# A two-layer attention encoder: order of the gate product, the raw keys' scaling and the second score halves in layer A

## The chip, the cores and the metric

The kernel runs on one core of a Trainium2 chip. The core has a matmul engine (TensorE, PE in the profile; its weight loads are shown apart as PEld), three engines for elementwise work (VectorE or DVE, ScalarE or ACT, GpSimd or POOL), and SyncE (SP), on whose queue nearly all DMA transfers of this kernel are issued. Each engine has a stream of its own instructions. Operands lie in SBUF, matmul results in PSUM. The metric is the device time of one execution in microseconds, lower is better; the median of a few runs is given.

## What is computed

The input x has 512 tokens of 1024 channels, all in float32. Two layers follow each other, each with 16 heads of 64 channels: RMS norm, one input projection to queries, keys, values and a gate, an attention, the product with silu(gate), an output projection, and the residual sum.

```
for i in range(2):
    hn = rms_norm(x, norm_gain[i])
    y = mixer_a(...) if i == 0 else mixer_b(...)
    x = x + y
```

Layer A (`mixer_a`) has three groups of queries, keys and values per head, with dilations 1, 4 and 16, and merges the three attentions by their softmax denominators; queries and keys are RMS-normalised per head. The part that matters here, for each head:

```
q = rms_norm(qkv[:, :, g, 0], q_gain[g])
k = rms_norm(qkv[:, :, g, 1], k_gain[g])
logits = einsum('...qd,...kd->...qk', q, k) * scale + bias      # masked to a window
p = exp(logits - max); out = (p @ v) / denom                    # per group g
y = sum(alpha[g] * out[g]) * silu(gate)
y @ w_out
```

Layer B (`mixer_b`) is a two-dimensional neighbourhood attention on an 8 x 64 grid of the tokens, with one group. The change does not touch it.

## The kernel before

**Precision.** The large products are made as three matmuls of a high and a low part (`mm3`): high x high, high x low, low x high. Weights come from memory in blocks `wraw`; ACT casts the high part `wh` (line 127), and DVE or POOL subtracts it to get the low part `wl` (line 131). Both have four buffers of 512 columns, and `wraw` has three of 1024. The projections use one such piece for each of the eight k-steps, 12 matmuls of 512 columns a step.

**Head pairs.** Layer A goes through eight head pairs, `hc` = 0 to 7. For each, the main stream (`main_a`) projects 512 columns with the keys and values of dilations 4 and 16 (`rawk`), then 512 columns with the three queries and the first keys (`rawq`), then the first values (`v0_a`) and the gate (`gate_a`). Evictions from PSUM are on line 458 (ACT); POOL squares, DVE sums, and `head_norm` computes the reciprocal root and multiplies the raw tile by it in place (line 295, four DVE instructions, 128x256 for `rawk`, 128x512 for `rawq`). For `rawk` the root is made on POOL (lines 108 to 120), which takes some microseconds.

**Two streams.** PE runs in an order written out by the program. A main stream yields the projections, matmul by matmul; a side stream yields the attention work (transposes, scores, product with v), and `run` puts pieces of the side stream between the projections' matmuls. A model clock (`clock`) adds up, in ticks of about a nanosecond, what PE's matmuls should take; it knows nothing of waits. The side stream says when it wants to go on: `yield 1200` means 1200 ticks later, `yield "wait", key, 5200` means 5200 ticks after the event `key` was stamped. `later_on(delay, job)` puts a job into a list of timers that `tick` starts once the model clock is there. What the program issues this way is its program order. The streams of the other engines are arranged by a planner that may move an instruction ahead of others; `keep_in_program_order` pins one behind the instruction that was issued on that engine just before it.

**The stage around the change.** Between the projections of head pair hc + 1 the side stream runs the attention of pair hc (`attn_a`), in two halves u = 0 and 1 of two query tiles each. Its order for pairs 0 to 5 ("moved" pairs) is:

- the projection `rawk` of pair hc + 1 ends and stamps its event; `normed` calls `head_norm`, which issues the root and the scaling (line 295);
- `split_q` prepares queries and keys (ACT lines 601 and 620, DVE lines 604 and 624);
- if the pair before has its product with v pending, it is taken now: `weigh` makes 48 matmuls into the tile `o`, and `put_y` multiplies the gate by it (line 673, DVE), casts the high part of y (line 679, ACT) and subtracts for the low part (line 680, POOL). This is so for hc = 1 to 5, as pair 0 has none before it;
- 5200 ticks after the stamp, `scores(0)`: 12 matmuls of the first group and 64 small ones of the other two, into four tiles "log", two for each query tile;
- softmax on DVE (lines 790, 801, 652) and ACT (lines 812, 653), then DVE transposes of the probabilities into the tile `tr` (line 725, one buffer); `send` writes `tr` to memory (line 734) and reads it back in another layout (line 738), by timers;
- 17800 ticks after the stamp, `scores(1)`, with the same behind it;
- 22500 ticks after the stamp, `k_a` transposes the normalised raw keys of pair hc + 1 on PE (tile "tp") and DVE scales them by the gains (line 525).

Pair 6 has `yield 1200` and `yield 8500` in place of the two waits, and pair 7 a path of its own. The tiles `o`, "log" and "tp" share a pool of four PSUM banks (`ps_side`, bufs=4), taken in turn, so a new tile waits until the one that had its bank is read. The projections have four other banks.

Of the kernel before, what the change touches and what calls it, by code (L numbers as in the profile page):

```python
# [26 lines left out]
NHC = 8  # L27
# [15 lines left out]
def tile_hybrid_encoder(  # L43
# [13 lines left out]
    nc = tc.nc  # L57
# [47 lines left out]
    def rsqrt(eng, r, ss, n, scale):  # L105
        v = wk.tile([P, 32], F32, tag="nv", name="nv", bufs=1)
        a = wk.tile([P, 32], F32, tag="na", name="na")
        eng.tensor_scalar(v[:, :n], ss, scale, EPS, op0=ALU.mult, op1=ALU.add)
        eng.tensor_scalar(
            r.bitcast(I32), v[:, :n].bitcast(I32), -0.5, float(0x5F3759DF), op0=ALU.mult, op1=ALU.add  # L110
        )
        for _ in range(3):
            eng.tensor_mul(a[:, :n], r, r)  # L113
            if eng is nc.vector:
                eng.scalar_tensor_tensor(a[:, :n], a[:, :n], -0.5, v[:, :n], op0=ALU.mult, op1=ALU.mult)
                eng.scalar_tensor_tensor(r, a[:, :n], 1.5, r, op0=ALU.add, op1=ALU.mult)
                continue
            eng.tensor_mul(a[:, :n], a[:, :n], v[:, :n])  # L118
            eng.tensor_scalar(a[:, :n], a[:, :n], -0.5, 1.5, op0=ALU.mult, op1=ALU.add)  # L119
            eng.tensor_mul(r, r, a[:, :n])  # L120
# [105 lines left out]
    def later_on(delay, job):  # L226

        timers.append((clock[0] + delay, job))
        timers.sort(key=lambda t: t[0])
# [46 lines left out]

    later = []

    def head_norm(raw, ss, ns, held):


        rs = wk.tile([P, 32], F32, tag="rs", name="rs")
        rsqrt(nc.vector if ns == 8 else nc.gpsimd, rs[:, : 4 * ns], ss[:, : 4 * ns], 4 * ns, 1.0 / DH)

        def scale():
            for i in range(4):
                by = rs[:, i * ns : (i + 1) * ns].unsqueeze(2)
                if len(raw.shape) == 4:
                    v = raw[:, :, i, :].rearrange("p (h a f) r -> p f h a r", h=2, f=4)
                    by = rs[:, i * ns : (i + 1) * ns].rearrange("p (f h) -> p f h", h=2)  # L290
                    by = by.unsqueeze(3).unsqueeze(4).to_broadcast([P, 4, 2, 2, 32])
                else:
                    v = raw[:, i, : ns * 64].rearrange("p (a b) -> p a b", b=64)
                    by = by.to_broadcast([P, ns, 64])
                m = nc.vector.tensor_mul(v, v, by)  # L295
                if held:
                    tc.keep_in_program_order(m)

        if held:
            later.append(scale)  # L300
        else:
            scale()

# [122 lines left out]
    def project_qk(n, ns, key, hc, guard, first=False, **kw):  # L426
# [38 lines left out]
        if first:  # L465
            st["first"] = raw, ss
            return
        normed(raw, ss, ns, key, hc)

    def normed(raw, ss, ns, key, hc):  # L470
        head_norm(raw, ss, ns, key == "raw")
        if key == "rawq" and moved(hc):
            turn_q(raw)
        st[key, hc] = raw
        stamp[key, hc] = clock[0]
# [54 lines left out]
    def turn_q(raw):  # L530

        for i in range(4):
            nc.vector.transpose(raw[:, :, i, :], raw[:, :, i, :])
# [121 lines left out]
    def put_y(hc, o, permuted, last):  # L655

        gt, rest = st.pop(("gate", hc))
        for _ in rest:
            pass
        if last and permuted:  # L660
            for c in range(4):
                q = slice(P * c, P * c + P)
                of = lambda t: t.rearrange("p (s x) -> p s x", x=16)[:, :, 4 * c : 4 * c + 4]
                nc.vector.tensor_mul(of(gt), of(gt), of(o))
                src = gt.rearrange("p (t ja x) -> p x ja t", t=4, ja=8)[:, 4 * c : 4 * c + 4]
                h, l = (t[:, hc, q].rearrange("p (x ja t) -> p x ja t", x=4, ja=8) for t in (st["y_h"], y_l))
                nc.scalar.copy(h, src)
                nc.vector.tensor_sub(l, src, h.bitcast(F32))
            return
        h, l, src = st["y_h"][:, hc, :], y_l[:, hc, :], gt  # L670
        if permuted:

            nc.vector.tensor_mul(gt, gt, o)
            src = gt.rearrange("p (t ja x) -> p x ja t", t=4, ja=8)
            h, l = (t.rearrange("p (x ja t) -> p x ja t", t=4, ja=8) for t in (h, l))
        else:
            for grid, line in ((mid_rc, mid_o), (edge_rc, edge_o)):
                nc.vector.tensor_mul(grid(gt), grid(gt), line(o))
        nc.scalar.copy(h, src)
        (nc.vector if last else nc.gpsimd).tensor_sub(l, src, h.bitcast(F32))  # L680
        stamp["ya" if permuted else "yb", hc, "y"] = 0
# [62 lines left out]
    def attn_a(hc):  # L744
# [7 lines left out]
        def scores(u):  # L752

            tiles = []
            for t in (2 * u, 2 * u + 1):
                cs, n = (64, 192) if t == 0 else (0, 192) if t == 3 else (0, 256)
                tiles.append((t, [bank("log") for _ in range(2)], cs, n))
            for t, lgs, cs, n in tiles:
                ks = slice(P * t + cs, P * t + cs + n)
                qs = slice(P * t, P * t + P)  # L760
                mm3_heads(
                    [lg[:, cs : cs + n] for lg in lgs],
                    lambda hs: q0h[hs, qs], lambda hs: q0l[hs, qs],
                    lambda hs: k0h[hs, ks], lambda hs: k0l[hs, ks], False,
                )
            for t, lgs, cs, n in tiles:
                for g in range(2):
                    for j in range(4):
                        for hd in range(2):
                            hs = slice(64 * hd, 64 * hd + 64)  # L770
                            matmul(
                                lgs[hd][32 * j : 32 * j + 32, 256 + P * g : 384 + P * g],
                                qt[hs, t, 1 + g, 32 * j : 32 * j + 32],
                                k12[hs, g, P * j : P * j + P],
                                share=2,
                                start=False,
                                stop=(g == 1),
                            )
            return [
                (hd, t, softmax(hd, t, lgs[hd], cs, n)) for t, lgs, cs, n in tiles for hd in range(2)  # L780
            ]
# [34 lines left out]
        def turn_p(hd, t, pr):  # L816
            tp = bank("tp")
            for i in range(4):
                transpose(tp[:, i * P : (i + 1) * P], pr[:, i * P : (i + 1) * P])
            dst = sb(pts[0], at(t, 0, hd, 0), [[32, 4], [512, 4], [1, 32]])  # L820
            nc.vector.tensor_copy(dst, tp.rearrange("p (i a r) -> p i a r", i=4, a=4))
# [25 lines left out]
        if hc < NHC - 1:  # L847
            for u in range(2):
                if moved(hc):
                    if pending and u == 0:  # L850
                        pending.pop(0)()
                        yield
                    yield "wait", ("rawk", hc + 1), 5200 if u == 0 else 17800
                else:
                    yield 1200 if u == 0 else 8500
                turned = turner(512)
                turners.append(turned)
                for hd, t, pr in scores(u):
                    turned.put(pr, 512, 256 * hd + 128 * (t % 2))
                send = partial(turned.send, pq[:, 2048 * u : 2048 * u + 2048], 8500, 1200)  # L860
                later_on(7000 + 2000 * u, send)
                if pending and u == 0:
                    yield 5000
                    pending.pop(0)()
            pending.append(lambda: put_y(hc, weigh(), True, False))
        else:
            for u in range(2):
                if u == 0:
                    yield "wait", ("gate", hc), 500
                yield 600  # L870
                held = scores(u)
                yield 3200
                if pending:
                    yield "wait", ("gate", hc - 1), 16800
                    pending.pop(0)()
                    yield
                for args in held:
                    turn_p(*args)
                    yield
            yield from v_a(hc)  # L880
            stamp["ya", "turned"] = 0
            put_y(hc, weigh(), True, True)
            yield

# [391 lines left out]
```

## Time and profile before

| | |
|---|---|
| median of 3 runs | 878.72 us (878.3 to 880.6) |
| profiled execution, as timed | 881.69 us |
| its span, first to last instruction | 879.9 us |
| mean granted PE clock | 0.984 |
| DMA, mean over the span | 161 GB/s |

The profiled execution is a run of its own, a little slower than the three. In the page's map of 40 slices one digit stands for 22 us; layer A fills the slices up to about 600 us, layer B the rest. "PEclk" is the clock that was granted to PE, as a share of full speed. In rows of waits, `X <- Y: a, n, m` means that instructions of X stood idle until Y had finished, for a us in total, n times, at most m us.

### The profile page before, as it was taken

The numbers are of one execution on the slowest core, as the hardware profiler recorded it, in microseconds if no ns is written. First come the engines' busy times: TensorE is split into PE (matmuls) and PEld (weight loads), VectorE is DVE, ScalarE is ACT, GpSimd is POOL, SyncE is SP. The second block draws the span as 40 slices with busy tenths as digits, with TensorE's granted clock in tenths as the row PEclk, the third lists the DMA queues.
The fourth block names the chain that finished last, engine by engine and source line by source line (L and its number), as shares of the span: only waits on it lengthen the run. The fifth ranks groups of instructions, "written<-read, shape, count | busy, mean of one in ns | idle before, by whom it ended". The sixth has DMA issues, their size and how long they took to land.

```text
span 879.9 us, 15373 instructions
## 1 busy us (share of the span) xinstructions
PE 855.7 (97%) x5547; PEld 711.0 (81%) x5547; DVE 522.9 (59%) x1335; ACT 430.6 (49%) x924; POOL 304.9 (35%) x493
## 2 busy tenths in 40 slices
PE   8999999899899899899999999999999999999998
PEld 6788878688688688688778778788988988889786
DVE  6354684574666567468357674538566666666743
ACT  7433654452652462463354543536366546665541
POOL 2252432442442432414414314112443345433511
PEclk9999999899999999999999999999999999999999
DMA  6346288268368358448638364156235655546223
GB/s 242 108 134 195 78 252 241 87 188 260 86 195 267 98 172 245 144 135 223 202 128 220 124 182 144 49 172 198 87 93 167 177 157 167 165 132 195 95 89 128
DMA packets 65372, 141.23 MB, mean 161 GB/s; under 512 B 5904, under 2 KB 23248, under 8 KB 65296
## 3 DMA queue, kind: packets, MB, share of 16 engines
q1 hardware_dynamic: 65008, 140.24, 52.2%
q8 instruction: 44, 0.72, 0.3%
q14 instruction: 32, 0.26, 0.1%
q10 hardware_dynamic: 288, 0.01, 0.0%
HBM read 109.11 MB, written 31.12 MB: 159 GB/s over the span
## 4 chain that ended last, share of the span: by engine, by line
PE 84%; DVE 5%; ACT 4%; POOL 3%; DMA 2%; issue 1%; SPq 0%; ACTq 0%; POOLq 0%; DVEq 0%
PE acc L206 72%; PE log L206 5%; PE tp L210 3%; PE o L206 3%; ACT rawk L458 2%; DVE rawk L295 1%; DMA qd<-rawq 1%; ACT p L1065 1%; POOL na L118 1%; ACT p L653 1%; POOL na L113 1%; DMA qt<-qd 1%; DMA hg<-in_head_gain 1%; POOL na L119 0%; POOL rs L120 0%
## 5 line engine op out<-in xcount | busy, mean ns | idle before, releaser
L127 ACT CAST wh<-wraw 128x512 fp32r<-128x512 f32 (+1 forms) x276 | 162.1, 588 | 304.8 <-PE acc L206 258.6
L206 PE MATMUL acc<-wh,hn_h 128*128 128x512 f32 (+1 forms) x768 | 297.0, 387 | 2.1 <-ACT wh L127 1.2
L206 PE MATMUL acc<-wl,hn_h 128*128 128x512 f32 (+1 forms) x768 | 288.0, 375 | 0.7 <-DVE wl L131 0.7
L206 PE MATMUL acc<-wh,hn_l 128*128 128x512 f32 (+1 forms) x768 | 288.1, 375 | 0.0
L131 POOL TENSOR_TENSOR wl<-wraw,wh 128x512 fp32r<-128x512 f32 (+1 forms) x110 | 136.8, 1243 | 367.4 <-ACT wh L127 337.3
L131 DVE TENSOR_TENSOR wl<-wraw,wh 128x512 fp32r<-128x512 f32 (+1 forms) x166 | 114.9, 693 | 156.3 <-ACT wh L127 151.9
L206 PEld LDWEIGHTS acc<-wh,hn_h 128*128 128x128 f32 x768 | 146.2, 190 | 31.4 <-issue 6.2
L206 PEld LDWEIGHTS acc<-wh,hn_l 128*128 128x128 f32 x768 | 145.8, 190 | 21.3
L206 PEld LDWEIGHTS acc<-wl,hn_h 128*128 128x128 f32 x768 | 146.4, 191 | 20.3 <-DVE wl L131 1.0
L206 PE MATMUL acc<-hn_h,wh 128*128 128x512 f32 x192 | 77.1, 402 | 1.6 <-ACT rawq L458 1.4
L206 PE MATMUL acc<-hn_l,wh 128*128 128x512 f32 x192 | 74.9, 390 | 0.0
L206 PE MATMUL acc<-hn_h,wl 128*128 128x512 f32 x192 | 74.9, 390 | 0.0
L653 ACT ACTIVATE p<-p,mn 128x512 f32<-128x512 f32 (+3 forms) x128 | 69.3, 586 | 0.0
L812 ACT ACTIVATE p<-p,mn 128x512 f32<-128x512 f32 (+1 forms) x64 | 44.8, 701 | 45.8 <-DVE mn L801 45.8
L273 DVE TENSOR_REDUCE ss<-sq 128x4 f32<-128x256 f32 (+1 forms) x96 | 48.3, 503 | 22.0 <-POOL sq L272 17.5
L725 DVE STREAM_TRANSPOSE tr<-p 128x512 f32<-128x512 f32 (+1 forms) x80 | 54.3, 686 | 9.7 <-ACT p L653 9.2
L272 POOL TENSOR_TENSOR sq<-rawk 128x256 f32<-128x256 f32 x64 | 40.5, 638 | 52.1 <-ACT rawk L458 44.2
L206 PE MATMUL acc<-y_h,wh 128*128 128x512 f32 x128 | 52.1, 407 | 0.0
L206 PE MATMUL acc<-y_h,wl 128*128 128x512 f32 x128 | 50.0, 391 | 0.0
L206 PE MATMUL acc<-y_l,wh 128*128 128x512 f32 x128 | 50.0, 391 | 0.0
L295 DVE TENSOR_TENSOR rawk<-rawk,rs 128x256 f32<-128x256 f32 x64 | 34.0, 591 | 22.7 <-POOL rs L120 22.3
L206 PEld LDWEIGHTS acc<-hn_h,wh 128*128 128x128 f32 x192 | 36.1, 188 | 11.7 <-ACT rawk L458 2.1
(138 smaller groups left out, 1098.3 us busy)
## 6 DMA issues: line engine op xcount, KB each, us to landing
wraw<-in_w SPq DMA_DIRECT2D x95, 512.0 KB
wraw<-in_w SPq DMA_DIRECT2D x38, 384.0 KB
td<-tr SPq DMA_DIRECT2D x14, 1024.0 KB
pt<-td SPq DMA_DIRECT2D x56, 256.0 KB
qd<-rawq SPq DMA_DIRECT2D x6, 1024.0 KB
qt<-qd SPq DMA_DIRECT2D x24, 256.0 KB
td<-tr SPq DMA_DIRECT2D x6, 896.0 KB
pt<-td SPq DMA_DIRECT2D x24, 224.0 KB
```

Of the source, the lines that this page charges most:

```text
L113: eng.tensor_mul(a[:, :n], r, r)
L127: nc.scalar.copy(h, raw)
L131: eng.tensor_sub(l, raw, h.bitcast(F32))
L206: nc.tensor.matmul(o, l, r, **kw)
L210: nc.tensor.transpose(o, i, ident)
L272: nc.gpsimd.tensor_mul(sq, v, v)
L273: nc.vector.tensor_reduce(ss[:, i * ns : (i + 1) * ns], sq.rearrange("p (a b) -> p a b", b=64), axis=AX.X, op=ALU.add)
L295: m = nc.vector.tensor_mul(v, v, by)
L458: nc.scalar.activation(dst, src, AF.Copy, scale=rs_n[:, i : i + 1])
L653: nc.scalar.activation(pr, pr, AF.Copy, scale=mn[:, 3:4])
L725: nc.vector.transpose(dst, src[:, :n].rearrange("p (i b k) -> p i b k", b=4, k=32))
L812: nc.scalar.activation(row, row, AF.Exp, bias=mn[:, 1:2], scale=-1.0, accum_out=mn[:, 2:3])
```

## The change

Four places change, and no arithmetic:

1. `put_y` pins the gate product of layer A (line 673) behind the DVE instruction issued just before it.
2. `head_norm` takes a delay. For `rawk` of head pairs 1 to 6 the four scaling multiplications (line 295) are issued by a timer 9000 ticks later, and pinned there; the reciprocal root stays where it is.
3. For pairs 0 to 5 the second half of the scores is wanted 16800 ticks after the stamp of `rawk`, not 17800.
4. For pair 6 the second half follows 7000 ticks after the first, not 8500.

```diff
-    def head_norm(raw, ss, ns, held):
+    def head_norm(raw, ss, ns, held, delay=0):
...
                 m = nc.vector.tensor_mul(v, v, by)
-                if held:
+                if held or delay:
                     tc.keep_in_program_order(m)
...
         if held:
             later.append(scale)
+        elif delay:
+            later_on(delay, scale)
         else:
             scale()
...
-        head_norm(raw, ss, ns, key == "raw")
+        head_norm(raw, ss, ns, key == "raw", 9000 if key == "rawk" and 0 < hc < NHC - 1 else 0)
...
-            nc.vector.tensor_mul(gt, gt, o)
+            tc.keep_in_program_order(nc.vector.tensor_mul(gt, gt, o))
...
-                    yield "wait", ("rawk", hc + 1), 5200 if u == 0 else 17800
+                    yield "wait", ("rawk", hc + 1), 5200 if u == 0 else 16800
                 else:
-                    yield 1200 if u == 0 else 8500
+                    yield 1200 if u == 0 else 7000
```

## Prediction

> **What bounds the kernel now.** I read the page first, for the busy shares of the engines and the granted clock along the span.
>
> ```profile
> span 879.9 us, 15373 instructions
> PE 855.7 (97%) x5547; PEld 711.0 (81%) x5547; DVE 522.9 (59%) x1335; ACT 430.6 (49%) x924; POOL 304.9 (35%) x493
> PEclk9999999899999999999999999999999999999999
> ```
>
> TensorE (PE) is busy 97% of the span, the next engine 59%. So time can come only from PE's 24 us of idle, or from busy PE that runs below its speed. The view of waits, for PE alone, says who causes the idle part:
>
> ```profile
> PE log L206 <- DVE gt L673: 13.6, 5, 2.8
> PE acc L206 <- ACT rawq L458: 2.1, 2, 1.4
> ```
>
> Over half of the idle time is five waits of the score matmuls ("log") for the gate product of line 673; the rest is mostly the start. The timeline of one of the five, VectorE (DVE) first, then PE (start, duration, engine, line, operation, count; in brackets the idle time before it and who ended it):
>
> ```profile
> 156.55 0.73 DVE L624 SCALAR_TENSOR_TENSOR q0l<-qt,gk,q0h 128x512 fp32r<-128x512 f32 x1
> 160.07 2.47 DVE L295 TENSOR_TENSOR rawk<-rawk,rs 128x256 f32<-128x256 f32 x4 [2.78 <-POOL rs L120]
> 162.47 0.67 DVE L673 TENSOR_TENSOR gt<-gt,o 128x512 f32<-128x512 f32 x1
> 156.67 1.47 PE L206 MATMUL o<-pt,v 128*64 128x256 f32 x12
> 160.06 0.30 PE L206 MATMUL log<-k0h,q0h 64*128 64x256 f32 x1
> 163.19 0.58 PE L206 MATMUL log<-k0h,q0h 64*128 64x256 f32 x1 [2.83 <-DVE gt L673]
> ```
>
> The product o is complete at 156.67 + 1.47 = 158.14. The first half of the scores takes four side banks of the pool's four, and o still holds one; the seven matmuls up to 160.06 fill three banks, the eighth needs o's. Line 673 would free it, but DVE's stream has the raw keys' scaling (line 295) ahead of it, which stands 2.78 us for GpSimd's reciprocal root and then takes 2.47. So a product that could start at 158.14 starts at 162.47.
>
> The wait costs more than its length. Windows from each release to the start of the second half's scores:
>
> ```profile
> core 0: us, PE busy (x) PEld busy (x) DVE busy (x) ACT busy (x) POOL busy (x), PEclk, DMA share, GB/s
> 163.19:178.62 15.43, 15.43 (x119) 12.27 (x119) 7.31 (x26) 8.61 (x17) 3.17 (x3) 0.81 0.35 117
> 233.38:247.72 14.34, 14.34 (x119) 11.45 (x119) 7.32 (x26) 8.48 (x17) 3.00 (x4) 0.88 0.36 126
> 302.06:316.32 14.26, 14.26 (x119) 11.44 (x119) 7.31 (x26) 8.49 (x17) 3.00 (x4) 0.88 0.34 119
> 370.66:386.44 15.78, 15.78 (x119) 12.54 (x119) 7.31 (x26) 8.60 (x17) 2.99 (x4) 0.79 0.33 116
> 440.76:455.17 14.41, 14.40 (x119) 11.37 (x119) 7.32 (x26) 8.64 (x17) 3.01 (x4) 0.88 0.37 126
> 163.20:169.20 6.00, 6.00 (x77) 4.74 (x78) 3.87 (x20) 3.85 (x9) 1.53 (x1) 0.51 0.00 0
> 98.60:104.00 5.40, 5.40 (x27) 4.48 (x25) 4.08 (x20) 1.66 (x5) 0.96 (x5) 1.00 0.28 96
> ```
>
> PE is busy throughout, but the granted clock is 0.79 to 0.88, and all of the loss lies in the first six us (0.51 in the first stage). The last row is the control: head pair 0 has the same scores and no product ahead of them, does not wait, and keeps 1.00.
>
> **The change part by part.** No instruction is added or removed; three things move.
>
> *Line 673 pinned, and line 295 issued 9000 ticks later (head pairs 1 to 6).* Nothing is then ahead of the product at 158.14: DVE finished line 624 at 157.28. It ends at 158.14 + 0.67 = 158.8, and the eighth matmul is due at about 160.1, with 1.3 us to spare. The five waits go: **13.6 us**. A pin can make DVE stand for o, up to 0.9 us from 157.28; behind it would stand the low-part splits and the softmax, of which the first has nothing to do there and the second needs scores not yet made.
>
> With the waits goes the clock loss that follows them: 15.43 x 0.19 + 14.34 x 0.12 + 14.26 x 0.12 + 15.78 x 0.21 + 14.41 x 0.12 = **11.4 us**. The same by work, from undisturbed rows:
>
> ```profile
> 209.76 10.95 PE acc L206 x48
> 97.02 0.30 PE L206 MATMUL log<-k0h,q0h 64*128 64x256 f32 x2
> 98.60 0.50 PE L206 MATMUL acc<-wh,hn_h 128*128 128x512 f32 x1
> ```
>
> The eighth score matmul of pair 0 starts near 97.09 and the projection resumes at 98.60, so 1.5 us; with 48 projection matmuls, 10.95, a stage needs 12.5. The five take 74.22 in sum: 74.2 - 62.3 = 11.9. I take 11.4. From below it is bounded by nothing (the loss has another cause, a rival below).
>
> *Where the scaling goes.* Four multiplications per head pair land behind the first half's softmax. The rows that say whether there is room:
>
> ```profile
> 99.92 1.43 DVE L295 TENSOR_TENSOR rawk<-rawk,rs 128x256 f32<-128x256 f32 x4 [2.48 <-POOL rs L120]
> 165.33 0.36 DVE L790 CUSTOM_DVE_ANT_0 p<-log,e 128x192 f32<-128x192 f32 x1 [2.19 <-PE log L206]
> 171.59 1.29 DVE L725 STREAM_TRANSPOSE tr<-p 128x512 f32<-128x512 f32 x2
> 175.92 0.69 DVE L131 TENSOR_TENSOR wl<-wraw,wh 128x512 fp32r<-128x512 f32 x1 [3.03 <-ACT wh L127]
> 178.68 0.69 DVE L131 TENSOR_TENSOR wl<-wraw,wh 128x512 fp32r<-128x512 f32 x1 [2.07 <-ACT wh L127]
> 180.18 0.42 DVE L790 CUSTOM_DVE_ANT_0 p<-log,e 128x256 f32<-128x256 f32 x1 [0.81 <-PE log L206]
> 184.07 0.60 PE L210 MATMUL tp<-ident,rawk 128*128 128x128 f32 x4
> ```
>
> The scaling costs 1.43 us (pair 0) to 2.47 us (pair 1). The softmax burst on DVE runs from 165.33 to 172.88, and until 180.18 DVE has only two splits, so some 5.9 us are free. Even with the second half 1.0 us nearer, 2.47 fits. The scaled keys are first read by PE at 184.07, 11 us after the burst. I cost it at **0**; without that cover it would be 1.43 to 2.47 us for each of six pairs.
>
> What could be late next is the supply of split weights, since ScalarE (ACT) is taken by the exponentials while PE now runs at full speed. Pair 0 again is the control, with pair 1 below it:
>
> ```profile
> 106.20 0.60 ACT L127 CAST wh<-wraw 128x512 fp32r<-128x512 f32 x1
> 170.26 0.60 ACT L127 CAST wh<-wraw 128x512 fp32r<-128x512 f32 x1
> 166.02 0.79 PE L206 MATMUL acc<-wh,hn_h 128*128 128x512 f32 x1
> ```
>
> In pair 0 the first cast after the scores comes 106.20 - 98.60 = 7.6 us after the projection resumes, because there the scaling stands ahead of the softmax; PE at clock 1.00 does not wait for it. In pair 1 it comes 170.26 - 166.02 = 4.2 us after, and the change leaves that distance, as both hang on the scores. Cost 0; from above, 2 us in each of five pairs.
>
> *Second halves 1000 ticks nearer (pairs 0 to 5), 1500 for pair 6.* This moves 12 + 64 score matmuls, the softmax behind them, and on SP's queue the second half's write of the transposed probabilities and its four reads, a little further ahead of weight loads. The single buffer "tr" has to be written out before the second half's transposes: that write leaves at 172.92, the transposes start at 184.31.
>
> ```profile
> 172.92 0.38 SPq L734 DMA_DIRECT2D td<-tr  x1
> 184.31 0.71 DVE L725 STREAM_TRANSPOSE tr<-p 128x512 f32<-128x512 f32 x1 [0.45 <-ACT p L653]
> 172.00:176.00 4.00, 4.00 (x20) 3.30 (x19) 0.97 (x3) 1.35 (x3) 1.63 (x2) 1.00 0.78 263
> 118.57 0.50 PE L206 MATMUL acc<-hn_h,wh 128*128 128x512 f32 x1 [1.37 <-ACT rawq L458]
> 117.85 0.66 ACT L458 ACTIVATE rawq<-acc,rs_n 128x512 f32<-128x512 f32 x1
> 498.34 0.50 PE L206 MATMUL acc<-wh,hn_h 128*128 128x512 f32 x1 [0.77 <-ACT rawq L458]
> ```
>
> 11.4 us apart; 1 MB at 263 GB/s is 4.0, so one us less is free. The gain is in pair 0: there PE waits 1.37 us because the query eviction sits in ACT behind the second half's exponentials. One us earlier, it gives back about **1.0** (bounds 0 and 1.37). The other such wait, at 498.34, lies in pair 6's first half, which does not move.
>
> **The sum.** The profiled execution took 881.69 us, 1.8 around its span of 879.9; the median shown is 878.72, the slowest of those runs 880.6. The stages' clock losses differ (1.7 to 3.3), so I read the 3 us between them as that loss falling out differently, and not as a term to keep: the sum starts from 881.69, whose waits I counted. 881.69 - 13.6 - 11.4 - 1.0 = **855.7 us**.
>
> **Rivals.**
> *A. Given back in part.* Short waits in place of the long ones: the product stretched by GpSimd's work beside it (one multiplication of line 295 took 1.47 us, the median is 0.418, minimum, median and maximum below), or a split behind the scaling. Up to 2 us in five pairs: 856 to 866, at 861. For it: ACT is full in the bursts. Against: pair 0.
>
> ```profile
> L295 DVE TENSOR_TENSOR rawk<-rawk,rs x64: 409/418/1504, 48.9 to 826.7; 128x256 f32<-128x256 f32 x64
> ```
>
> *B. The waits go, the clock loss stays.* Then 881.69 - 13.6 - 1.0 = 867.1. Were it tied to the dense stretch after the scores and not to the idle, pair 0 would show it; it does not, and five of five waits do. The Trainium skill, page "TensorE: Matmul & The Clock Gate", section "HAM oscillation — how this bites in real kernels", speaks for this rival: it lets PE idle up to about 3.4 us without a slower clock, and these waits are shorter. By that rule the sum would be B's; the trace disagrees, 0.51 after 2.83 us.
>
> *C. The change doesn't do what it says*: something else on DVE keeps the product late, such as the instruction it is pinned behind. Time as before, 878 to 881.
>
> *D. Slower.* The scaling falls behind the second half's softmax, whose DVE burst ends with the transpose below. The key transposes, due at 184.07, would then wait till 188.79 + 1.43 or + 2.47, 6.2 to 7.2 us, in six pairs: 37 to 43, and 2.3 of clock in each (11.4 / 5), 14. Net of the 26 gained, 907 to 913. It decides once the scaling ends after 184.07; the delays put it 7800 ticks ahead of the second half, which speaks against it.
>
> ```profile
> 188.10 0.69 DVE L725 STREAM_TRANSPOSE tr<-p 128x512 f32<-128x512 f32 x1
> ```
>
> **How the numbers follow.** Forecast (853 to 859): 0.73. A beyond 859: 0.14. B: 0.05. C: 0.03. D: 0.03. Below 853: 0.02. Both bounds of the known terms (11.9 and 1.37) give 854.8; A's end gives 866. The range is 853 to 866. A measurement of this kernel tells 0.3%, some 2.6 us, from no change: slower 0.03 (D), same 0.03 (C), faster 0.94.
>
> **What would show it.** Right: no wait of "log" for line 673; line 673 within 0.7 us of o's end and ahead of line 295; granted clock 1.00 from 100 us to the end of layer A; line 295 between the first and the second half's line 790; PE busy near 844 us. Wrong: windows of layer A still below 1.00 with no wait ahead of them (B), PE waits on lines 131, 127 or on "tp" (A, D).

## The result, and the profile after

| | before | changed |
|---|---|---|
| median on one chip | 879.28 us (878.3 to 880.6, 4 runs) | 854.09 us (852.59 to 854.65, 4 runs) |
| profiled execution, as timed | 881.69 us | 854.65 us |
| its span | 879.9 us | 852.7 us |
| mean granted PE clock | 0.984 | 1.000 |

The ratio is 0.971, with a 95% interval of 0.9691 to 0.9729. The forecast of 855.7 us lies 1.6 above the measured median.

The lines of the changed kernel's page that answer to those of the kernel before (its lines stand two lower in the file from line 300 on, so 673 is now 675, and 458 is 460):

```profile
span 852.7 us, 15400 instructions
PE 843.6 (99%) x5547; PEld 702.7 (82%) x5547; DVE 520.2 (61%) x1335; ACT 431.3 (51%) x924; POOL 307.1 (36%) x493
```

Two of the four runs of the changed kernel, the profiled one among them, have a mean clock of 1.000, the other two 0.997.

The same matmuls now keep PE busy for 843.6 us, not 855.7. Most of the 12 us that went is the clock loss of the five stages, 11.4 us by the prediction's windows. The view of PE's waits has lost its longest row:

```profile
PE acc L206 <- ACT rawq L460: 1.4, 2, 0.8
PE o L206 <- DMA eb<-lb_d: 0.9, 1, 0.9
PE busy L358 <- DVE warm L346: 0.9, 1, 0.9
PE acc L206 <- ACT wh L127: 0.9, 1, 0.9
```

The view lists no wait of "log" for the gate product any more. The timeline of the same stage as in the prediction, DVE:

```profile
155.20 0.75 DVE L626 SCALAR_TENSOR_TENSOR q0l<-qt,gk,q0h 128x512 fp32r<-128x512 f32 x1
156.74 0.69 DVE L675 TENSOR_TENSOR gt<-gt,o 128x512 f32<-128x512 f32 x1 [0.79 <-PE o L206]
166.12 1.29 DVE L727 STREAM_TRANSPOSE tr<-p 128x512 f32<-128x512 f32 x2
167.34 2.46 DVE L295 TENSOR_TENSOR rawk<-rawk,rs 128x256 f32<-128x256 f32 x4
171.57 0.42 DVE L792 CUSTOM_DVE_ANT_0 p<-log,e 128x256 f32<-128x256 f32 x1 [1.18 <-PE log L206]
```

PE in the same stage:

```profile
158.62 0.30 PE L206 MATMUL log<-k0h,q0h 64*128 64x256 f32 x2
176.84 0.60 PE L210 MATMUL tp<-ident,rawk 128*128 128x128 f32 x4
```

And windows over three of the five stages (busy time of PE, its weight loads, DVE, ACT and POOL, then the granted clock, the DMA share and GB/s):

```profile
156.70:171.00 14.30, 14.30 (x152) 11.38 (x160) 10.29 (x31) 8.46 (x17) 5.72 (x10) 1.00 0.26 91
221.00:235.00 14.00, 13.93 (x132) 10.93 (x133) 11.66 (x33) 8.85 (x18) 5.72 (x7) 1.00 0.23 80
285.00:299.00 14.00, 14.00 (x134) 10.88 (x132) 10.21 (x31) 8.46 (x17) 5.77 (x13) 1.00 0.22 77
```

DVE now stands for the product with v (0.79 us) and multiplies the gate at once. The two 256-column matmuls at 158.62, of which the second stood 2.83 us before, run together. The scaling costs its 2.46 us between the first half's last transposes and the second half's first reduction, for which DVE still has to stand 1.18 us. It ends at 169.80, 7 us ahead of the key transposes at 176.84. The clock is 1.00.

One of the five stages, that of pair 2, is not quite clean in this execution. Its product o is complete at 220.82, but DVE's stream has two low-part splits ahead of the gate product, and the first of them stood for ACT:

```profile
220.69 1.10 DVE L606 TENSOR_TENSOR k0l<-qt,k0h 128x512 fp32r<-128x512 f32 x1 [3.13 <-ACT k0h L603]
222.38 0.67 DVE L675 TENSOR_TENSOR gt<-gt,o 128x512 f32<-128x512 f32 x1
222.74 0.75 PE L206 MATMUL log<-k0h,q0h 64*128 64x256 f32 x2
```

The product ends at 223.05, and the two 256-column matmuls take 0.75 us where they take 0.30 in the other four stages: some 0.4 us that the view of waits does not list. The clock stays at 1.00 behind it, as the second window shows.

### The profile page after: what moved, and what is told of

It reads as the page before. It is cut to its first block, busy times and chain, and to the rows that moved or that the text cites. A ratio compares the mean times of both kernels' runs of the same rounds, so it can differ in the third digit from the quotient of the medians.

```text
span 852.7 us, 15400 instructions
## 1 busy us (share of the span) xinstructions
PE 843.6 (99%) x5547; PEld 702.7 (82%) x5547; DVE 520.2 (61%) x1335; ACT 431.3 (51%) x924; POOL 307.1 (36%) x493
## 4 chain that ended last, share of the span: by engine, by line
PE 87%; ACT 4%; DMA 4%; DVE 3%; issue 1%; POOL 1%; SPq 0%; ACTq 0%; POOLq 0%; DVEq 0%
PE acc L206 74%; PE log L206 5%; PE o L206 5%; PE tp L210 3%; DMA qd<-rawq 1%; ACT p L655 1%; ACT p L814 1%; DMA rp<-in_rpb 1%; ACT p L1067 1%; DMA qt<-qd 1%; POOL sq L270 1%; ACT wh L127 1%; DMA hg<-in_head_gain 0%; DVE wl L131 0%; DMA eb<-lb_d 0%
## 5 line engine op out<-in xcount | busy, mean ns | idle before, releaser
L131 DVE TENSOR_TENSOR wl<-wraw,wh 128x512 fp32r<-128x512 f32 (+1 forms) x166 | 111.1, 670 | 135.8 <-ACT wh L127 131.5
L206 PEld LDWEIGHTS acc<-hn_h,wl 128*128 128x128 f32 x192 | 36.0, 188 | 7.7
```

Of the source, the lines that this page charges most:

```text
L131: eng.tensor_sub(l, raw, h.bitcast(F32))
L206: nc.tensor.matmul(o, l, r, **kw)
```

## The experiments

Two theories stood against the forecast's own, that one order on DVE cost both the waits and the clock behind them: that the clock loss had another cause (rival B), and that one of the other edits carried the gain. All edits are shown against the changed kernel.

### Which edit does it

The pin alone (the delay and the nearer halves taken back):

```diff
-        head_norm(raw, ss, ns, key == "raw", 9000 if key == "rawk" and 0 < hc < NHC - 1 else 0)
+        head_norm(raw, ss, ns, key == "raw")
...
-                    yield "wait", ("rawk", hc + 1), 5200 if u == 0 else 16800
+                    yield "wait", ("rawk", hc + 1), 5200 if u == 0 else 17800
...
-                    yield 1200 if u == 0 else 7000
+                    yield 1200 if u == 0 else 8500
```

> Only the pin on the gate product; scaling and second halves as before. Order theory: the scaling (line 295) is issued before the product and stays ahead of it on DVE, so the five waits of 2.7 us and the clock loss behind them stay: 878 to 881 us, granted clock 0.98. Rival, the pin does the work: about 855 us, clock 1.00.

Measured: 880.43 us, ratio to the kernel before 1.0009 (0.9995 to 1.0024). No effect. In its timeline of DVE the scaling is still ahead of the product:

```profile
159.38 2.47 DVE L295 TENSOR_TENSOR rawk<-rawk,rs 128x256 f32<-128x256 f32 x4 [2.49 <-POOL rs L120]
161.78 0.68 DVE L675 TENSOR_TENSOR gt<-gt,o 128x512 f32<-128x512 f32 x1
```

and in its view of PE's waits the five of before are there:

```profile
PE log L206 <- DVE gt L675: 13.7, 5, 2.8
```

A pin holds an instruction behind what was issued before it; the scaling was issued before it, so the pin has nothing to lift it over the scaling.

The delay alone (product not pinned, second halves as before):

```diff
-            tc.keep_in_program_order(nc.vector.tensor_mul(gt, gt, o))
+            nc.vector.tensor_mul(gt, gt, o)
...
-                    yield "wait", ("rawk", hc + 1), 5200 if u == 0 else 16800
+                    yield "wait", ("rawk", hc + 1), 5200 if u == 0 else 17800
...
-                    yield 1200 if u == 0 else 7000
+                    yield 1200 if u == 0 else 8500
```

> Only the delay of the scaling; product not pinned, second halves as before. Order theory: with the scaling gone from ahead of it, the product starts when o is done, no pin needed: 855 us (the 854.1 of the whole change and 0.8 for the query eviction's wait of head pair 0), clock 1.00. Rival, the pin is needed as well: some waits of line 675 stay, 860 to 880 us.

Measured: 857.33 us, ratio 0.9749 (0.9723 to 0.9775), clock 0.999. Its timeline has the order of the whole change, without the pin:

```profile
156.15 0.69 DVE L675 TENSOR_TENSOR gt<-gt,o 128x512 f32<-128x512 f32 x1 [0.47 <-PE o L206]
166.75 2.45 DVE L295 TENSOR_TENSOR rawk<-rawk,rs 128x256 f32<-128x256 f32 x4
```

So the delay alone takes all five waits away, and the pin on the gate product is not needed. (The delayed multiplications keep the pins of their own that come with the delay.) The time was 2 us above what was expected.

The nearer second halves alone (no pin, no delay):

```diff
-            tc.keep_in_program_order(nc.vector.tensor_mul(gt, gt, o))
+            nc.vector.tensor_mul(gt, gt, o)
...
-        head_norm(raw, ss, ns, key == "raw", 9000 if key == "rawk" and 0 < hc < NHC - 1 else 0)
+        head_norm(raw, ss, ns, key == "raw")
```

> Only the second halves nearer; no delay, no pin. Order theory: worth the shorter wait of one query eviction, 0.8 us: 878 to 880 us, the five waits of 2.7 us unchanged. Rival, the second halves carry part of the gain: below 876 us.

Measured: 877.33 us, ratio 0.9979 (0.9962 to 0.9997), just below the band expected. The five waits stay (13.5 us). The gain is 878.38 - 877.33 = 1.1 us, at the edge of what these runs can tell: the interval ends just below 1.

Pin and delay, second halves as before (both `yield` lines back to 17800 and 8500):

> Pin and delay, second halves as before. Order theory: 855 us, the whole change less 0.8, with PE's wait on line 460 back at 2.1 us. Rival, the scaling needs the nearer second halves to be hidden: new waits of PE on lines 131 or 527, above 857 us.

Measured: 857.44 us, ratio 0.9743 (0.9721 to 0.9766). No PE wait on line 527 is new and the wait on 131 is the 0.4 us of the start, so the scaling is hidden without the nearer halves; yet the time stands 3 us above the whole change, which had run on another chip. That was repeated with both on one chip:

> The changed kernel as it is, on the same chip as the next three, to size what the nearer second halves are worth on top of pin and delay: 853 to 856 us.

> Pin and delay alone, second halves as before, beside the whole change on one chip. If the second halves are worth only the query eviction's wait (line 460, 2.1 to 2.6 us against 1.4) and the one wait of the query transposes: 1 to 2 us more than the whole change. If their worth is the 3.3 us by which pin and delay stood above 854.1 on another chip: 3 us or more.

Measured: 853.93 us for the whole change (ratio 0.9697, 0.9683 to 0.9711), 857.16 us for pin and delay (0.9738, 0.9723 to 0.9753). So by medians the nearer halves are worth some 3 us on top of the rest, and not 1. The view of PE's waits of pin and delay (the first of the two runs) shows about two of them:

```profile
PE acc L206 <- ACT rawq L460: 2.6, 3, 1.4
PE tp L210 <- DVE mn L803: 0.9, 1, 0.9
```

Against the whole change's rows above: 1.2 us more on line 460, among them a wait that the kernel before did not have, and 0.9 on pair 7's query transposes, which wait for a bank while DVE reduces pair 6's second half. Together 2.1 us. The rest is not settled by a row. The start of the kernel differs between executions by more than that, as the chain that ended last shows, first of the whole change (start, duration):

```profile
7.32 27.46 PE acc L206 x113
96.41 2.00 PE log L206 x75
```

and then of pin and delay in the second run:

```profile
7.29 25.91 PE acc L206 x113
94.83 2.00 PE log L206 x75
```

The same first matmuls took 27.46 us and 25.91 us. From pair 0's first scores to the end of the span it is 852.1 - 96.41 = 755.7 and 853.3 - 94.83 = 758.5 us: 2.8 apart. The two traces taken before these give 852.7 - 96.00 = 756.7 and 855.6 - 97.36 = 758.2, only 1.5 apart. So the nearer halves are worth between 1.5 and 3.2 us here, and what the view of waits does not show stays open.

### What a wait costs: idle time put back by itself

To separate the clock loss from the order of before, the changed kernel was given n reductions of o ahead of the gate product on DVE. Their results are not used, and nothing else in the program changes. The products taken in the stages of pairs 6 and 7 get them too.

```diff
+    scr = cp.tile([P, 8], F32, name="scr")
...
+            for _ in range(n):
+                tc.keep_in_program_order(
+                    nc.vector.tensor_reduce(scr, o.rearrange("p (a b) -> p a b", b=64), axis=AX.X, op=ALU.add)
+                )
             tc.keep_in_program_order(nc.vector.tensor_mul(gt, gt, o))
```

n = 2: 

> The changed kernel with two idle reductions of o (results unused) pinned ahead of the gate product on DVE, for a wait of a chosen length with nothing else moved. At some 0.65 us each they fill the product's margin of 1.3 us: PE waits 0 to 0.2 us in five stages. Both theories: 854 to 856 us, clock 1.00.

n = 4: 

> As with two, four idle reductions: a wait of about 1.3 us in five stages, 6.5 us. If the clock falls with any wait: 854 + 6.5 + 5 = 866 us or more. If only a wait near the length of the old ones lowers it: 861 us at clock 1.00.

n = 6: 

> Six idle reductions: a wait of about 2.6 us in five stages, 13 us, nearly that of the kernel before, with the raw keys' scaling where the change puts it. If the clock loss follows the idle time: 854 + 13 + 11 = 878 us, clock 0.98. Rival B, the loss has another cause in the order before: 867 us, clock 1.00.

n = 8: 

> Eight idle reductions: a wait of about 3.9 us in five stages, 19.5 us. If the clock loss follows the idle time: 854 + 19.5 + 11 to 17 = 885 to 891 us, with windows behind the wait at 0.8 or below in all five stages. Rival B: 874 us, clock 1.00.

Measured, with PE's waits of "log" for the gate product (line 680 in these kernels) and the mean clock of the profiled execution:

| n | time | runs | waits | mean clock |
|---|---|---|---|---|
| 2 | 858.21 us | 857.84 to 858.58 | 0.9 us (1, in pair 6's stage) | 0.997 |
| 4 | 873.29 us | 868.3 to 880.88 | 10.4 us (6) | 0.986 |
| 6 | 889.3 us | 889.14 to 889.46 | 18.2 us (6) | 0.983 |
| 8 | 899.8 us | 899.26 to 900.33 | 29.1 us (7) | 0.979 |

A reduction took 0.72 us, not 0.65, and pair 6's stage adds a wait that the expectation left out; so the waits, and the times, are longer than expected. With two, the view misses short waits in the other five stages. There the two 256-column matmuls take 0.63 us, as in this row, and not 0.30, so PE loses about 0.3 us in each:

```profile
159.06 0.63 PE L206 MATMUL log<-k0h,q0h 64*128 64x256 f32 x2
```

With the 0.9 us listed that is about 2.5 of the 4.1 us by which the time stands above that of the changed kernel (854.09); the rest is open. With four and six, the late product also puts evictions in ACT late, and PE waits for these too: 2.16 and 2.14 us with four, 1.98 us with six, each with a clock of 0.81 in the 9 us behind it. So the times contain more than the waits of the table. What matters is the clock behind the waits. With six, idle time of nearly the old length is back with the scaling where the change puts it, and the time is above that of the kernel before, by ratio 1.0108 (1.0067 to 1.0149). Windows of 9 us from each release, n = 6:

```profile
161.89:170.89 9.00, 9.00 (x101) 7.42 (x102) 6.63 (x27) 7.21 (x15) 1.92 (x2) 1.00 0.01 2
233.09:242.09 9.00, 9.00 (x90) 7.24 (x91) 5.81 (x24) 6.65 (x14) 1.54 (x1) 0.68 0.01 3
303.01:312.01 9.00, 9.00 (x95) 7.23 (x96) 6.42 (x26) 7.30 (x15) 1.58 (x2) 0.81 0.01 2
371.87:380.87 9.00, 9.00 (x95) 7.26 (x96) 5.99 (x25) 6.96 (x15) 1.54 (x1) 0.81 0.01 2
440.66:449.66 9.00, 9.00 (x89) 7.15 (x90) 5.81 (x24) 6.66 (x14) 1.53 (x1) 0.64 0.01 2
```

Four of five waits of 2.88 us lower the clock, as the five of before did. Rival B falls: the loss comes with the idle time, and not with the old order.

With four, two waits of nearly the same length in the timeline of PE:

```profile
159.09 0.35 PE L206 MATMUL log<-k0h,q0h 64*128 64x256 f32 x1 [1.42 <-DVE gt L680]
229.07 0.35 PE L206 MATMUL log<-k0h,q0h 64*128 64x256 f32 x1 [1.43 <-DVE gt L680]
```

and the windows behind them:

```profile
159.09:168.09 9.00, 9.00 (x101) 7.42 (x102) 6.63 (x27) 7.21 (x15) 1.91 (x2) 1.00 0.01 2
229.07:238.07 9.00, 9.00 (x95) 7.14 (x96) 6.79 (x27) 7.30 (x15) 1.57 (x2) 0.81 0.01 3
```

One costs its 1.42 us and no more, the other 9 x 0.19 = 1.7 us besides. In that execution two of the four such waits lowered the clock. It fits that eight runs of this one program spread over 12.6 us: their mean clocks run from 0.986, in the slowest, to 0.998, in the two fastest.

### Scaling later still, and a last adjustment

```diff
-        head_norm(raw, ss, ns, key == "raw", 9000 if key == "rawk" and 0 < hc < NHC - 1 else 0)
+        head_norm(raw, ss, ns, key == "raw", 20000 if key == "rawk" and 0 < hc < NHC - 1 else 0)
```

> The whole change with the scaling 20000 ticks later, not 9000, so that on DVE it stands behind the second half's transposes. Rival D of the prediction made real: the key transposes on PE are due 5 us ahead of the burst's end; waits of some 6.7 us for line 295 in six pairs, 40 us, and 2.3 of clock each, 14: about 908 us (895 to 915), slower than before. If the key transposes had room to spare: 854 to 860 us.

Measured: 860.62 us (860.1 to 861.14), ratio 0.9777 (0.9757 to 0.9797): 6.7 us above the whole change on the same chip, and not 54. The expectation was wrong by its place in the stream. The timeline, first two rows from head pair 0's stage, then three from pair 1's:

```profile
119.56 0.71 DVE L727 STREAM_TRANSPOSE tr<-p 128x512 f32<-128x512 f32 x1 [0.42 <-ACT p L655]
120.19 2.24 DVE L295 TENSOR_TENSOR rawk<-rawk,rs 128x256 f32<-128x256 f32 x4
183.01 1.52 DVE L295 TENSOR_TENSOR rawk<-rawk,rs 128x256 f32<-128x256 f32 x4
184.38 0.60 PE L210 MATMUL tp<-ident,rawk 128*128 128x128 f32 x4
184.52 0.68 DVE L727 STREAM_TRANSPOSE tr<-p 128x512 f32<-128x512 f32 x1
```

The only wait of PE for the scaling, of head pair 0's stage:

```profile
PE tp L210 <- DVE rawk L295: 4.4, 1, 4.4
```

and the window behind it:

```profile
121.50:130.50 9.00, 8.92 (x35) 6.95 (x36) 7.22 (x20) 1.82 (x3) 3.33 (x3) 0.81 0.42 109
```

Only in pair 0's stage does the scaling come behind all four transposes. There the mechanism of rival D is seen at its full price for one stage: 4.4 us of wait and 1.7 of clock, 6.1 of the 6.7. In pair 1's stage the planner let the scaling run ahead of the transposes of the second half, just in time, and PE did not wait; a pin holds only behind the one instruction issued before it.

```diff
-                    yield "wait", ("rawk", hc + 1), 5200 if u == 0 else 16800
+                    yield "wait", ("rawk", hc + 1), 5200 if u == 0 else 15800 if hc == 0 else 16800
...
-                    yield 1200 if u == 0 else 7000
+                    yield 400 if u == 0 else 7000
```

> The whole change, with the second half of pair 0 another 1000 ticks nearer and the first half of pair 6 800 ticks nearer, aimed at the last two waits for query evictions (0.62 and 0.77 us). If these hang on the softmax burst ahead of the eviction as the second halves' did: 1.2 us less than the whole change, line 460 gone from PE's waits. If the moves only put other work late: no difference.

Measured: 853.22 us (850.83 to 856.64), ratio 0.9696 (0.9672 to 0.972) beside 0.9697 for the whole change. PE's wait on line 460 fell from 1.4 to 0.43 us, one wait of that length, so the moves do what they were meant to; the time shows no difference that these runs can tell.

## Why the prediction was right, and where its sum was off

*The five waits, 13.6 us.* Right, but for some 0.4 us in pair 2's stage of the profiled execution. There the gate product starts 1.56 us behind the end of o, where the prediction had asked for 0.7. The waits are gone in the changed kernel, gone with the delay alone, and all there (13.7 us) with the pin alone. The cause named, scaling ahead of the product on DVE, was the right one; of the two edits that the prediction put together, the delay does it, and the pin does nothing measurable.

*The clock behind them, 11.4 us.* Right. PE's busy time fell from 855.7 to 843.6 (844 forecast), the clock is 1.00 in the stages, and idle time put back by itself brings the loss back. The reading that all of it lies in the first six us holds for four of the five stages; in the window from 370.66 us, 3.0 of the 3.3 us do. The mean of 1.000 is not had in every run: in a trace of the same kernel with 0.997, the loss lies in the first 20 us (0.86 and 0.97 in the first two tens), ahead of anything that changed.

The Trainium skill, page "TensorE: Matmul & The Clock Gate", section "HAM oscillation — how this bites in real kernels", whose rule was the support of rival B, lets PE idle for about 3.4 us; here waits of 1.42 to 1.43 us lowered the clock in two of four cases, so the measurement decides against it. The same page of the Trainium skill, section "Part 1: The HAM clock gate (the "warmup" mystery)", has a window of some 3.4 us that runs freely, and half the clock when it falls. By that figure one window at half clock would cost half of 3.4, or 1.7 us, an estimate; the smallest loss seen here where the clock fell, 9 x (1 - 0.81) = 1.7 us, agrees.

*The scaling at no cost.* Right: 2.46 us between the halves, no PE wait behind it.

*The nearer second halves, 1.0 us.* This is the term that was mis-sized. The eviction's wait in pair 0 gave 0.75 (1.37 to 0.62), inside its bounds. The prediction missed the 0.9 us that PE waited for DVE's reductions ahead of pair 7's query transposes, which is gone wherever the second halves are nearer (pair 6's come 1500 ticks earlier). It also missed that without the nearer halves an eviction wait of 0.5 to 0.6 us appears in pin and delay once the other waits are gone. Measured beside pin and delay: 857.16 - 853.93 = 3.2 us by medians, 2.8 and 1.5 by the two pairs of spans behind the start; waits show 2.1. By itself, without pin and delay, the edit gave the 1 us that was forecast.

*The sum.* From pair 0's first scores to the end, 879.9 - 96.68 = 783.2 us before and 852.7 - 96.00 = 756.7 after: 26.5 us, where the terms were 26.0. The other 0.7 us of the 27.2 between the spans lie in the start, ahead of anything that changed. That the terms fit the medians as well is in part luck. The profiled execution of the kernel before lost more clock than most: its mean is 0.984, and 19 runs on one chip have a median of 0.988. By medians pin and delay bring 878.38 - 857.44 = 20.9 us on that chip and 880.22 - 857.16 = 23.1 on another, less than the 25.0 of the first two terms, while the nearer halves bring more than their 1.0. The two differences nearly cancel.

*The rivals.* A: in the changed kernel's profile it is seen only as the 0.4 us of pair 2's stage, behind late splits, and not as up to 2 us in five. B: refuted by n = 6. C: true of the pin by itself, which leaves the product where it was. D: its mechanism exists, as pair 0's stage with 20000 ticks shows, but the price was set too high, since it took a pin for a place behind the whole burst; the measured price was one stage's.

## What to carry to other kernels

A wait of PE on an engine off the critical path is to be priced by the wait and by the granted clock in the window behind it; here the second was nearly as large as the first. Where an instruction with a late input stands in an in-order stream ahead of one that frees a buffer, issue it later, beyond that one; a pin on the second instruction lifts it over nothing that was issued before it. Before such an order is tuned by microseconds, look at how far two profiles of one program differ ahead of the place that changes.

## What the runs showed of the hardware that was not expected

The clock loss comes in steps and in part by chance. By windows of 9 us behind the release it was none, 1.7 us or between 2.1 and 3.3 us, in the kernel before, in the pin alone, in the nearer halves alone and with n = 4 to 8; waits of one length had different losses. It also sets in at waits half as long as those of the kernel before. The waits of PE of at least 0.3 us that the timelines of all traces of this case list, from 100 us on:

| PE's wait | cases | clock lower behind it |
|---|---|---|
| 0.32 to 1.37 us | 62 | 0 |
| 1.42 to 1.43 us | 4 | 2 |
| 1.56 to 2.38 us | 6 | 6 |
| 2.65 to 2.88 us | 20 | 19 |
| 3.84 to 5.29 us | 8 | 8 |

The 20 waits are those of the kernel before, the pin alone, the nearer halves alone and the first five of n = 6. So a wait just under 1.4 us cost its length alone here, and one a little longer had a price that differs from run to run. A kernel with many of them spreads: 12.6 us with n = 4, against 2.1 us for the four runs of the changed kernel.
